# Turning the normed rows of two tiles in place, and a lower rate for the finish: a decoder layer on one core

## The chip, the cores and the metric

The kernel runs on one core of one Trainium2 chip. The core has TensorE (matrix products and transposes), VectorE, ScalarE and GpSimd, an on-chip memory of 128 partitions, and PSUM, where TensorE leaves its results in banks of 128 x 512 numbers. Transfers between the on-chip memory and DRAM run on 16 DMA engines; this kernel issues them from SyncE's queue (SP) and from ScalarE's. The metric is the device time of one execution in microseconds (us); lower is better.

## The reference

The kernel computes one decoder layer on 2048 rows of 1024 numbers, in float32. Cut to what matters:

```python
hn = rms_norm(h, mix_pre_g)
proj = hn @ w_in                                  # q, k, v and the input of a convolution group
attn_out = sliding_window_attention(q, k, v, attn_sinks, rel_bias)
conv_out = conformer_conv(u, ...)                 # GLU, 31 causal taps, LayerNorm, swish, pointwise
mixed = concatenate([attn_out, conv_out]) @ w_out
h = h + rms_norm(mixed, mix_post_g)
hn = rms_norm(h, ffn_pre_g)                       # the "normed rows" of this change
ff = (silu(hn @ w_gate) * (hn @ w_up)) @ w_down
h = h + rms_norm(ff, ffn_post_g)
```

with `rms_norm(x, g) = x * rsqrt(mean(x*x) + eps) * g`.

## The kernel before

**Tiles and stages.** The 2048 rows go in four tiles of 512 (tile 0 to 3), each of four blocks of 128 rows. A name carries its stage: `hl@G` is a buffer of the pool `hl` written in stage G. The stages are

- A: input projections of a tile; B: its attention; C: its convolution. The 31 taps of C run on VectorE over a long time, `stage_tail` does the rest.
- U: the pointwise weights are folded into the output projection, once.
- W (`stage_w`, lines 693 to 745): output projection of a tile in two groups of four 128-column blocks of the mixed rows. `norm_w` (747 to 784) follows: it scales the result, adds x, stores h to `h_scr`, takes the second mean square and writes the normed rows into `xs`, four buffers of the pool `chl`. Each block of normed rows then goes to DRAM (`hn_scr`, line 783) on ScalarE's queue.
- H (`stage_h_plain`, 824 to 835, and `stage_h_sums`, 837 to 867): the normed rows have to stand with their columns on the partitions. `turned` (806 to 811) loads a column block of a tile from `hn_scr` (`load_cols`, line 788: 128 partitions x 4 pieces of 128 numbers) and turns it on TensorE in four transposes into one PSUM bank. `stage_h_plain` does this for the first tile of a pair (0 or 2): copy with the gain into a buffer of `gb`, store that to `hT` (line 831), then split into a high part (ScalarE, line 833) and a low part (VectorE, `lo`). It makes the operands B11 (column blocks 0 to 3) and B21 (4 to 7). `stage_h_sums` reads `hT` of the first tile back, turns the second tile of the pair (1 or 3) and makes the other operands.
- F (`stage_pre`, `stage_p1`): gate and up projections of a pair of tiles by a seven-product scheme of Strassen's kind; `stage_pre` does the products that need only B11 and B21. G (`stage_p2`): the down projection of the pair, in seven types of product, each over eleven steps; the splits of its operands are `hl@G` (line 792). When a type is complete, results for a pair of blocks go to `finish` (1088 to 1108): squares (ScalarE, L1094), products with the gain (GpSimd), a load of h from `h_scr` (L1102) into `chl` (first pair), the sum and the stores to `out`.

All products are in three parts (high x high, high x low, low x high).

**Order.** The program is written as generators that yield a pace in us. One main line (A0 to A3, W1, F, G, F, G) drives clocks, and beside it run lanes: `lw` (W0, and during the first pair's G: C2, W2, C3, W3, B11.2, then N3, the norm of tile 3), `lh` (H of the pairs), `lf` (finishes), `lc` (taps), and others. Each lane has a rate, which may depend on the name of the item at its head (`rates`): an item that yields 2.0 at a rate of 1.25 takes 1.6 us of the main line. `until` runs a lane's items to the end of the named one at once. This fixes the order in which instructions are emitted; a planner then orders each engine's queue by emission priority and by its own estimate of when data and buffers are there, so an instruction may run well ahead of its place in the program. On the chip each engine, and each of the queues, works in order: a DMA issue that waits holds back what is behind it on its engine.

**Buffers that the change touches.** `chl` has five buffers: in `norm_w` one holds the gain and four hold `xs`; W's second group, `finish` and `stage_h_sums` use the same pool. `gb` has two (the turned row on its way to `hT`), `ct` is one PSUM bank (turned blocks of C and of H's first tiles), `fa` four, `fc` three, `at` two.

**Where W0 and W2 lie.** W0 with its norm ends with A3, right ahead of W1, which is the main line's next item; W1's second group waits until eight products of F have run (`Q0 = 8`, line 735 to 740). W2 runs in lane `lw` beside the first pair's G.

Of the kernel before, what the change touches and what calls it, by code (L numbers as in the profile page):

```python
# [12 lines left out]
F32 = mybir.dt.float32  # L13
# [4 lines left out]
AF = mybir.ActivationFunctionType  # L18
# [7 lines left out]
P = 128  # L26
T = 512
NT = S // T
KC = D // P
# [8 lines left out]
def layer_kernel(ctx, tc, x, xT, cols, rows, sinks, relb, onehot, w_in, w_pw, w_out, w_gate, w_up, w_down, out):  # L38
    nc = tc.nc
# [4 lines left out]
    dr = ctx.enter_context(tc.tile_pool(name="dr", bufs=1, space=DRAM))  # L44

    uid = [0]
    lab = ["X0"]
# [7 lines left out]
    def t_(tag, shape, dt=F32):  # L55
        return sb.tile(list(shape), dt, tag=tag, name=nm(tag), bufs=BUFS[tag])

    def f4(tag, shape=(P, D)):
        return t_(tag, shape)

    def f2(tag, shape=(P, T)):
        return t_(tag, shape)

    def hl(tag):
        return t_(tag, (P, 2, T), F32R)

    def sm(n, dt=F32):
        kind = "A" if lab[0][0] == "G" else lab[0][0]
        return sb.tile([P, 8], dt, tag="sm" + kind, name=nm("sm"), bufs=16)[:, 0:n]

    def bank(tag, bufs):
        return ps.tile([P, T], F32, tag=tag, name=nm(tag), bufs=bufs)
# [3 lines left out]
    ct = lambda: bank("ct", 1)  # L76


    act = nc.scalar.activation
# [54 lines left out]
    def weight(src, low, made, raw=None, on_pool=True):  # L134
        if raw is None:
            raw = t_("raw", (P, 2, T))
            nc.sync.dma_start(raw, src)
        return [split_w(raw[:, n], "w", low[n], made, on_pool) for n in range(2)]
# [55 lines left out]
    ident = cst.tile([P, P], F32, name="ident")  # L194
# [16 lines left out]
    g_ffn = colt[:, 8:16]  # L211
# [29 lines left out]
    glu_scr = dr.tile([4, P, S], F32, name="glu_scr")  # L241
    hn_scr = dr.tile([S, D], F32, name="hn_scr")
    y_scr = dr.tile([4, P, S], F32, name="y_scr")
    qs = {}
    started = set()

# [433 lines left out]
    def block_half(acc, units, n, first, L, bank_of, s0=0):  # L680
        cs = slice(n * T, (n + 1) * T)
        for i in range(len(acc)):
            s = i + s0
            lab[0] = L
            o = bank_of()
            three(o, [((a[s // 4][:, 0, ss(s)], a[s // 4][:, 1, ss(s)]), (w[:, 0], w[:, 1])) for a, w in units])
            if first:
                act(acc[i][:, cs], o, AF.Copy)
            else:
                vtt(acc[i][:, cs], acc[i][:, cs], o, ALU.add)  # L690
            yield 0.65 * len(units)

    def stage_w(w, atag, htags, rtags, bank_of, norm=None, ready=None):
        G = KC // len(htags)
        L = f"W{w}"
        lab[0] = L
        acc = [f4(atag) for _ in range(4)]

        def acts(gi):
            aa = []  # L700
            lab[0] = L
            n = 4 if rtags[gi] == "yt" else 2
            for c in range(G * gi, G * gi + G, n):
                ms = t_(rtags[gi], (P, n, T))
                nc.sync.dma_start(ms, mixT[c : c + n, :, w * T : (w + 1) * T].rearrange("c p t -> p c t"))
                for j in range(n):
                    a = hl(htags[gi])
                    act(a[:, 0], ms[:, j], AF.Copy)
                    vtt(a[:, 1], ms[:, j], a[:, 0].bitcast(F32), ALU.subtract)
                    aa.append([a])  # L710
            return aa

        def weights(gi, n):
            ws = []
            for c in range(G * gi, G * gi + G, 2):
                if c < 4:
                    ws += weight(w_out[c : c + 2, :, n * T : (n + 1) * T].rearrange("c p t -> p c t"), lo_out[n, c : c + 2], w > 0, on_pool=False)
                else:
                    for j in range(2):
                        ws.append(hl("w"))  # L720
                        nc.sync.dma_start(ws[-1].bitcast(F32), fold[n, c - 4 + j])
            return ws

        nxt = acts(0)
        yield W_LEAD
        for gi in range(KC // G):
            aa = nxt
            for n in range(2):
                lab[0] = L
                if n == 1 and gi + 1 < KC // G and not (ready and G * gi + G == 4):  # L730
                    nxt = acts(gi + 1)
                ws = weights(gi, n)
                yield from block_half(acc, list(zip(aa, ws)), n, gi == 0, L, bank_of)
            if ready and G * gi + G == 4:
                for i, c in enumerate(ready()):
                    if i == Q0 // 2:
                        ld.until("C1")
                        lab[0] = L
                        nxt = acts(gi + 1)
                    yield c  # L740
        tail = norm_w(w, acc)
        if norm:
            norm(tail)
        else:
            yield from tail

    def norm_w(w, acc):
        L = f"W{w}"
        lab[0] = L

        def whole(src):
            t = f4("chl")
            nc.sync.dma_start(t, src)
            return t

        gb = whole(rows[0].partition_broadcast(P))
        ssq = sm(4)
        for s in range(4):
            act(junk, acc[s], AF.Square, accum_out=ssq[:, s : s + 1])
            yield 0.75  # L760
            lab[0] = L
        r = rsqrt(ssq, 4, D, w < 3)
        xs = [whole(x[w * T + s * P : w * T + (s + 1) * P]) for s in range(4)]
        ssq2 = sm(4)
        yield 3
        for s in range(4):
            lab[0] = L
            stt(acc[s], acc[s], r[:, s : s + 1], gb, ALU.mult, ALU.mult)
            yield 1.25
            lab[0] = L  # L770
            vtt(acc[s], xs[s], acc[s], ALU.add)
            r0 = w * T + s * P
            nc.sync.dma_start(h_scr[r0 : r0 + P], acc[s])
            act(junk, acc[s], AF.Square, accum_out=ssq2[:, s : s + 1])
            yield 1.25
        lab[0] = L
        r2 = rsqrt(ssq2, 4, D, w < 3)
        yield 3
        for s in range(4):
            lab[0] = L  # L780
            act(xs[s], acc[s], AF.Copy, scale=r2[:, s : s + 1])
            r0 = w * T + s * P
            nc.scalar.dma_start(hn_scr[r0 : r0 + P], xs[s])
            yield 1.25

    def load_cols(w, k, tag):
        t = f2(tag, (P, 4, P))
        nc.sync.dma_start(t, hn_scr[w * T : (w + 1) * T, k * P : (k + 1) * P].rearrange("(s p) c -> p s c", p=P))
        return t
# [5 lines left out]
    def lo(x, w, on_pool):  # L795
        (ptt if on_pool else vtt)(w[:, 1], x, w[:, 0].bitcast(F32), ALU.subtract)
# [7 lines left out]
    COLTAG = {0: ["fc", "at", "fc", "at"], 2: ["fc", "at", "fc", "at"]}  # L804

    def turned(w, k, bank_of, tag):
        c = load_cols(w, k, tag)
        b = bank_of()
        for s in range(4):
            nc.tensor.transpose(b[:, s * P : (s + 1) * P], c[:, s], ident)  # L810
        return b

    def op_tile(ws, ops, n, k, spare):
        tag = OPTAG[ws[0]][n][k]
        if tag == "yt":
            if "yt" not in spare:
                spare["yt"] = t_("yt", (P, 2, 2, T), F32R)
            w = spare["yt"][:, k]
        else:
            w = hl(tag)  # L820
        ops.setdefault(n, []).append(w)
        return w

    def stage_h_plain(ws, ops, n, off):
        L = f"H{ws[0]}"
        for k in range(4):
            lab[0] = L
            b = turned(ws[0], k + off, ct, COLTAG[ws[0]][k] if ws[0] else "fa")
            u = f2("gb")
            act(u, b, AF.Copy, scale=g_ffn[:, k + off : k + off + 1])  # L830
            nc.scalar.dma_start(hT[ws[0] // 2][k + off], u)
            o = op_tile(ws, ops, n, k, {})
            act(o[:, 0], u, AF.Copy)
            lo(u, o, False)
            yield 2.0
# [499 lines left out]
    lf = Lane(1.2, 0)  # L1335
    lh = Lane(1.2, 0)
# [2 lines left out]
    ld = Lane(2.0, 0)  # L1339
    lanes = [lb, lc, lu, lw, ld, lf, lh, lt]  # L1340
    lh.rates = {"N1": 1.2, "S0": 0.9, "H0": 1.2}
    lc.rates = {"T0": RC0, "T1": RC1, "T2": RC2, "T3": RP}
    lw.rates = {"W0": RW0, "C2": RW, "W2": RW, "C3": RW, "W3": RW}

# [57 lines left out]
            hn_a[t + 1] += split_x(t + 1, xa[t + 1][0], xa[t + 1][2], range(4, KC))  # L1402
    lw.until("W0")
    mids = [dr.tile([7, NF // 2, P, T], F32, name=f"mids{i}") for i in range(2)]
    hT = [dr.tile([KC, P, T], F32, name=f"hT{i}") for i in range(2)]
    td = dr.tile([4, NF // 2, P, T], F32, name="td")
    keeps = [dr.tile([PRES[2 * i], P, T], F32, name=f"keeps{i}") for i in range(2)]
    ws, ops = (0, 1), {}
# [12 lines left out]
    ws, ops = (2, 3), {}  # L1421
# [76 lines left out]
```

## Time and profile before

| | |
|---|---|
| time, median of 3 runs | 1985.41 us (1983.29, 1985.41, 1989.40) |
| profiled execution | 1988.67 us; its span in the trace 1986.6 us |
| mean granted clock of TensorE in it | 0.992 |
| busiest engines, share of the span | TensorE 97%, VectorE 73%, ScalarE 48%, GpSimd 17% |
| moved by DMA | 454.56 MB, mean 229 GB/s |
| DMA packets | 229403, of them under 512 B 22632, under 2 KB 48400 |
| stores to hn_scr | 16 of 512 KB, from 476.8 to 1297.7 us |
| loads from hn_scr for tile 0 | 8 of 256 KB into `fa`, from 489.1 to 518.2 us |

How to read it: times are from the start of the span. In a row of a timeline stand start, length, engine, line, operation, `out<-in`, shape and count; a bracket gives the idle time ahead of it and what ended that. SPq and ACTq are the queues' DMA issues, which are not counted as busy. In the waits, a row is the waiting instruction, what it waited for, total us, number of times and the longest. In the DMA issues, the last number is the median time from issue to landing.

### The profile page before, as it was taken

The numbers are of one execution on the slowest core, as the hardware profiler recorded it, in microseconds if no ns is written. First come the engines' busy times: TensorE is split into PE (matmuls) and PEld (weight loads), VectorE is DVE, ScalarE is ACT, GpSimd is POOL, SyncE is SP. The second block draws the span as 40 slices with busy tenths as digits, with TensorE's granted clock in tenths as the row PEclk, the third lists the DMA queues.
The fourth block names the chain that finished last, engine by engine and source line by source line (L and its number), as shares of the span: only waits on it lengthen the run. The fifth ranks groups of instructions, "written<-read, shape, count | busy, mean of one in ns | idle before, by whom it ended". The sixth has DMA issues, their size and how long they took to land.

```text
span 1986.6 us, 26669 instructions
## 1 busy us (share of the span) xinstructions
PE 1930.2 (97%) x8730; PEld 1542.3 (78%) x8730; DVE 1460.2 (73%) x2578; ACT 955.2 (48%) x1878; POOL 336.4 (17%) x415
## 2 busy tenths in 40 slices
PE   8999999998999999899999999989999999999997
PEld 6777767776777778778888778768888888888886
DVE  5999969986875898888658975766666665455557
ACT  5455454436737633334355466556634433345443
POOL 4011111003121200000000110144423332311003
PEclk9999999999999999999999999989999999999999
DMA  8797757669659867885477788797844542466664
GB/s 312 253 316 234 228 176 242 213 198 306 203 191 353 290 216 237 285 267 181 154 236 251 266 302 282 270 315 244 289 149 165 170 164 81 143 232 194 210 196 144
DMA packets 229403, 454.56 MB, mean 229 GB/s; under 512 B 22632, under 2 KB 48400, under 8 KB 229264
## 3 DMA queue, kind: packets, MB, share of 16 engines
q1 hardware_dynamic: 211024, 426.64, 64.5%
q10 hardware_dynamic: 18240, 26.22, 3.6%
q8 instruction: 69, 1.13, 0.2%
q14 instruction: 70, 0.57, 0.1%
HBM read 331.65 MB, written 121.12 MB: 228 GB/s over the span
## 4 chain that ended last, share of the span: by engine, by line
PE 43%; DMA 10%; DVE 9%; issue 3%; POOL 2%; ACT 2%; SPq 1%; DVEq 0%; ACTq 0%; POOLq 0%
PE mm@F L85 29%; PE mm@G L85 12%; DVE fc@C L94 2%; PE tr@W L85 2%; DMA gb@F<-keeps 1%; DVE hl@G L94 1%; DMA mids<-fa@F 1%; DMA fa@G<-mids 1%; DMA td<-fc@G 1%; DVE w@F L94 1%; DMA fc@G<-w_down 1%; DMA wx@G<-w_down 1%; DVE fa@F L94 1%; DVE chl@F L94 1%; DMA mixT<-fc@C 1%
## 5 line engine op out<-in xcount | busy, mean ns | idle before, releaser
L94 DVE SCALAR_TENSOR_TENSOR fc@C<-glu@C,colt,fc@C 128x512 f32<-128x512 f32 x480 | 356.5, 760 | 2.9
L85 PE MATMUL mm@F<-hl@H,w@F 128*128 128x512 f32 x1056 | 253.0, 390 | 3.3 <-ACT mm@F L919 2.0
L85 PE MATMUL mm@G<-hl@G,hl@G 128*128 128x512 f32 x924 | 232.6, 397 | 11.2 <-ACT hl@G L792 7.7
L85 PEld LDWEIGHTS mm@F<-hl@H,w@F 128*128 128x128 f32 x1056 | 197.5, 188 | 46.3 <-ACT mm@F L919 3.7
L85 PEld LDWEIGHTS mm@G<-hl@G,hl@G 128*128 128x128 f32 x924 | 173.0, 190 | 51.7 <-ACT hl@G L792 9.0
L85 PE MATMUL mm@A<-hl@A,w@A 128*128 128x512 f32 x840 | 206.5, 395 | 4.2 <-ACT w@A L127 1.9
L792 ACT ACTIVATE w@F<-chl@F 128x512 fp32r<-128x512 f32 x220 | 135.4, 625 | 142.1 <-PE mm@F L85 131.5
L85 PE MATMUL mm@G<-w@G,hl@G 128*128 128x512 f32 x876 | 199.4, 389 | 0.0
L85 PEld LDWEIGHTS mm@G<-w@G,hl@G 128*128 128x128 f32 x876 | 164.4, 188 | 34.1
L85 PEld LDWEIGHTS mm@A<-hl@A,w@A 128*128 128x128 f32 x840 | 155.4, 188 | 42.2 <-ACT w@A L127 2.6
L94 DVE TENSOR_TENSOR w@F<-chl@F,w@F 128x512 fp32r<-128x512 f32 x198 | 144.8, 735 | 35.9 <-ACT w@F L792 35.3
L85 PE MATMUL mm@F<-ql@H,w@F 128*128 128x512 f32 x528 | 128.4, 391 | 9.2 <-ACT mm@F L1026 5.0
L85 PE MATMUL mm@F<-mid@H,w@F 128*128 128x512 f32 x528 | 131.7, 396 | 0.0
L85 PE MATMUL mm@F<-p@H,w@F 128*128 128x512 f32 x528 | 129.4, 390 | 0.0
L85 PE MATMUL mm@F<-x@H,w@F 128*128 128x512 f32 x528 | 125.7, 391 | 0.0
L85 PEld LDWEIGHTS mm@F<-ql@H,w@F 128*128 128x128 f32 x528 | 98.8, 188 | 31.6 <-ACT mm@F L1026 6.4
L494 POOL TENSOR_SCALAR_AFFINE_SELECT p@B<-p@B 128x512 f32<-128x512 f32 x62 | 57.6, 938 | 374.0 <-ACT p@B L492 372.7
L85 PEld LDWEIGHTS mm@F<-mid@H,w@F 128*128 128x128 f32 x528 | 100.0, 190 | 21.9 <-ACT fa@F L1047 0.5
L85 PEld LDWEIGHTS mm@F<-p@H,w@F 128*128 128x128 f32 x528 | 99.5, 188 | 21.0 <-ACT at@F L1040 0.2
L85 PEld LDWEIGHTS mm@F<-x@H,w@F 128*128 128x128 f32 x528 | 98.6, 188 | 21.5 <-issue 0.8
L127 ACT ACTIVATE w@A<-raw@A 128x512 fp32r<-128x512 f32 x110 | 67.4, 625 | 93.5 <-PE mm@A L85 54.8
L94 DVE TENSOR_TENSOR w@G<-raw@G,w@G 128x512 fp32r<-128x512 f32 x73 | 51.5, 705 | 68.1 <-ACT w@G L792 66.8
(302 smaller groups left out, 3300.6 us busy)
## 6 DMA issues: line engine op xcount, KB each, us to landing
mids<-fa@F SPq DMA_DIRECT2D x154, 256.0 KB, 2.8
raw@A<-w_in SPq DMA_DIRECT2D x55, 512.0 KB, 4.7
w@A<-lo_in SPq DMA_DIRECT2D x84, 256.0 KB, 3.6
fc@G<-mids SPq DMA_DIRECT2D x77, 256.0 KB, 3.5
fa@G<-mids SPq DMA_DIRECT2D x75, 256.0 KB, 4.6
gb@F<-keeps SPq DMA_DIRECT2D x72, 256.0 KB, 3.9
w@W<-fold SPq DMA_DIRECT2D x32, 512.0 KB, 5.1
chl@F<-w_gate SPq DMA_DIRECT2D x22, 512.0 KB, 4.1
```

The source lines that it names most:

```text
L85: r = nc.tensor.matmul(*args, **kw)
L94: r = op(*args, **kw)
L127: act(w[:, 0], raw, AF.Copy)
L494: nc.gpsimd.affine_select(out=pg[:, kb].rearrange("p (i q) -> p i q", q=P), in_=pg[:, 1].rearrange("p (i q) -> p i q", q=P), compare_op=AL ...
L792: act(w[:, 0], x, AF.Copy)
```

## The change

Three things change.

1. Tile 0: `norm_w` no longer stores the normed rows to `hn_scr` (only odd tiles do). The four `chl` buffers are kept in `normed`, and `stage_h_plain` turns each column block straight from them (`turn_row`): four transposes into `ct`, one copy with the gain into `gb`, one store to `hT`, as before, but without the load. In `stage_w` of tile 1, B21.0 is run to its end ahead of the second group's splits, which want `chl`.
2. Tile 2: its eight column blocks are turned at the end of `norm_w(2)` in lane `lw`, 2.0 of pace each, and go to `hT` only. `stage_h_plain` of the second pair then loads each block from `hT` in place of turning it; the split stays.
3. Lane `lf`: the finishes of the first pair (O0.1, O0.3, E0.1, E0.3) run at a rate of 0.5 in place of 1.2; 1.2 is set again for the others.

Tiles 1 and 3 keep their way through `hn_scr`. `hT` is allocated earlier, without effect of its own.

```diff
+    hT = [dr.tile([KC, P, T], F32, name=f"hT{i}") for i in range(2)]
...
                     if i == Q0 // 2:
                         ld.until("C1")
+                        lh.until("B21.0")
                         lab[0] = L
                         nxt = acts(gi + 1)
...
             act(xs[s], acc[s], AF.Copy, scale=r2[:, s : s + 1])
-            r0 = w * T + s * P
-            nc.scalar.dma_start(hn_scr[r0 : r0 + P], xs[s])
+            if w % 2:
+                r0 = w * T + s * P
+                nc.scalar.dma_start(hn_scr[r0 : r0 + P], xs[s])
             yield 1.25
+        if w == 0:
+            normed.extend(xs)
+        if w == 2:
+            for k in range(KC):
+                turn_row(w, xs, k)
+                yield 2.0
+
+    normed = []
+
+    def turn_row(w, xs, k):
+        lab[0] = f"H{w}"
+        b = ct()
+        for s in range(4):
+            nc.tensor.transpose(b[:, s * P : (s + 1) * P], xs[s][:, k * P : (k + 1) * P], ident)
+        u = f2("gb")
+        act(u, b, AF.Copy, scale=g_ffn[:, k : k + 1])
+        nc.scalar.dma_start(hT[w // 2][k], u)
+        return u
...
         for k in range(4):
             lab[0] = L
-            b = turned(ws[0], k + off, ct, COLTAG[ws[0]][k] if ws[0] else "fa")
-            u = f2("gb")
-            act(u, b, AF.Copy, scale=g_ffn[:, k + off : k + off + 1])
-            nc.scalar.dma_start(hT[ws[0] // 2][k + off], u)
+            if ws[0]:
+                u = f2(COLTAG[ws[0]][k])
+                nc.sync.dma_start(u, hT[ws[0] // 2][k + off])
+            else:
+                u = turn_row(0, normed, k + off)
+                lab[0] = L
             o = op_tile(ws, ops, n, k, {})
             act(o[:, 0], u, AF.Copy)
             lo(u, o, False)
...
+    lf.rates = {n: 0.5 for n in ("O0.1", "O0.3", "E0.1", "E0.3")} | {n: 1.2 for n in ("Y0", "Y1", "O2.1", "O2.3")}
...
-    hT = [dr.tile([KC, P, T], F32, name=f"hT{i}") for i in range(2)]
```

## The prediction

> **What bounds the kernel now.** I read the page first, then the timeline of TensorE over the whole span for its idle stretches, then the same stretches on the other engines, in the stretch table and in the waits.
>
> ```profile
> PE 1930.2 (97%) x8730; PEld 1542.3 (78%) x8730; DVE 1460.2 (73%) x2578; ACT 955.2 (48%) x1878; POOL 336.4 (17%) x415
> ```
>
> TensorE is busy for 1930.2 of 1986.6 us, so all its idle time is 56 us, and the change takes no product away. It can gain only where TensorE stands still. Two long holes, the longest after the start, lie where the change works (timeline of TensorE: start, length, line, operation, count, and in brackets the idle time before):
>
> ```profile
> 491.45 1.65 PE L85 MATMUL tr@B<-kz,ql@A 64*128 64x256 f32 x12 [5.59 <-DVE sm@B L454]
> 493.03 7.45 PE L85 MATMUL mm@W<-w@W,hl@W 128*128 128x512 f32 x28
> 502.91 4.86 PE L85 MATMUL mm@W<-w@W,hl@W 128*128 128x512 f32 x20
> 510.22 0.97 PE L85 MATMUL tr@B<-kz,ql@A 64*128 64x256 f32 x11
> ...
> 1318.33 8.49 PE L85 MATMUL mm@G<-hl@G,hl@G 128*128 128x512 f32 x24 [6.50 <-ACT hl@G L792]
> 1328.90 5.74 PE L85 MATMUL mm@G<-hl@G,hl@G 128*128 128x512 f32 x24
> 1335.52 7.55 PE L85 MATMUL mm@G<-hl@G,hl@G 128*128 128x512 f32 x32 [0.88 <-DVE hl@G L94]
> ```
>
> After each hole the products run slowly for a while; the stretch table shows why. Its columns: stretch, length, busy time of TensorE, weight load, VectorE, ScalarE and GpSimd, then the granted clock, the DMA share and GB/s.
>
> ```profile
> 484.00:488.00 4.00, 1.87 (x17) 1.26 (x15) 3.93 (x7) 1.12 (x2) 0.00 (x0) 0.99 1.03 395
> 488.00:492.00 4.00, 0.55 (x4) 0.58 (x6) 4.00 (x15) 1.31 (x3) 0.00 (x0) 0.50 1.04 382
> 492.00:496.00 4.00, 4.00 (x21) 3.23 (x18) 3.96 (x8) 0.88 (x2) 0.00 (x0) 0.66 1.13 332
> ...
> 1312.00:1316.00 4.00, 0.00 (x0) 0.00 (x0) 0.00 (x0) 0.62 (x2) 0.00 (x0) 0.74 1.08 365
> 1316.00:1320.00 4.00, 1.67 (x4) 1.40 (x5) 3.34 (x3) 4.00 (x12) 3.82 (x4) 0.50 1.09 355
> 1320.00:1324.00 4.00, 4.00 (x10) 3.12 (x10) 3.90 (x7) 3.36 (x9) 3.83 (x6) 0.50 0.77 213
> ```
>
> The clock falls to 0.50. The 28 products at 493.03 take 7.45 us; at the later 4.86 / 20 = 0.243 us each they would take 6.80, and 12 of tr@B at 0.97 / 11 each 1.06 instead of 1.65: 1.24 us lost. The 24 products at 1318.33 lose 8.49 - 5.74 = 2.75. So the first hole is worth 5.59 + 1.24 = 6.83 us, the second 6.50 + 2.75 = 9.25, and the small one at 1335.52 another 0.88: 16.96 us for everything in reach. In both holes the DMA share is above 1.00: the transfers are the queue.
>
> **The first hole, tile 0.** What goes here: four stores to hn_scr on ScalarE's queue and eight loads from it on SP's. The 32 transposes, eight copies and eight hT stores stay.
>
> ```profile
> 476.84 0.34 ACTq L783 DMA_DIRECT2D hn_scr<-chl@W  x1
> 480.59 0.67 ACTq L783 DMA_DIRECT2D hn_scr<-chl@W  x1
> ...
> 476.66 0.38 SPq L607 DMA_DIRECT2D mixT<-fc@C  x1
> 480.55 0.37 SPq L705 DMA_DIRECT2D yt@W<-mixT  x1
> ...
> 483.66 0.55 DVE L94 TENSOR_SCALAR fc@C<-glu@C,colt 128x512 f32<-128x512 f32 x1 [7.43 <-DMA mixT<-fc@C]
> 490.69 2.19 ACT L708 ACTIVATE hl@W<-yt@W 128x512 fp32r<-128x512 f32 x4 [4.69 <-DMA yt@W<-mixT]
> ...
> hn_scr<-chl@W ACTq DMA_DIRECT2D x16, 512.0 KB, 6.7
> mixT<-fc@C SPq DMA_DIRECT2D x16, 256.0 KB, 5.2
> yt@W<-mixT SPq DMA_DIRECT2D x4, 1024.0 KB, 5.8
> hT<-gb@H ACTq DMA_DIRECT2D x16, 256.0 KB, 4.4
> ```
>
> The four stores are 2.1 MB, at 390 GB/s 5.4 us of all DMA engines, between 476.8 and 480.6. In the same time the store that VectorE waits for (its fc buffer) takes 483.66 - 476.66 = 7.0 us, 1.8 over its median, and the load that W1's products wait for takes 490.69 - 480.55 = 10.1 us, 4.3 over its median. Without the stores I set both at their medians: VectorE goes on 1.8 us sooner and gives TensorE its tr bank 1.8 us sooner.
>
> The rows are ready by 480, so the transposes may go into the hole instead of into the crowded time from 500 on (the first two rows below, of TensorE and of the stretch table, are a short hole from elsewhere):
>
> ```profile
> 803.93 1.66 PE L85 MATMUL mm@F<-yt@H,w@F 128*128 128x512 f32 x6 [1.65 <-DVE gb@F L94]
> ...
> 806.00:810.00 4.00, 4.00 (x20) 3.27 (x18) 4.00 (x7) 0.00 (x0) 0.00 (x0) 1.00 0.70 196
> ...
> 507.60 0.60 PE L810 MATMUL ct@H<-ident,fa@H 128*128 128x128 f32 x4
> 509.55 0.69 ACT L830 ACTIVATE gb@H<-ct@H,colt 128x512 f32<-128x512 f32 x1
> ```
>
> One turned row costs 0.60 us on TensorE, 4.8 us in all. There is one ct bank and there are two gb buffers, each held until its hT store has landed (4.4 us), so I let three rows into the hole: 1.8 us. The hole shrinks to 5.59 - 1.8 - 1.8 = 2.0 us. A hole of 1.65 us, the nearest, is followed by a clock of 1.00, so I charge none: -3.6 - 1.24 = **-4.8 us**. Bounds: 0 if the earlier hT stores fill the gap that the hn_scr stores leave, -6.83 if the hole closes; a loss only by the third rival. ScalarE saves four issues. The four chl buffers stay taken until the eighth row is turned; behind them waits only W1's second split, whose products come after eight products of the next stage (8 x 2.76 us in the code's own pace). The forced end of B21.0 ahead of that split finds it done: 16 units at rate 1.2 are 13.3 us, against 4 + 20.8 us of pace before that point. Both cost nothing; without that cover the price is a row's whole turn, 0.60 + 0.69 + 4.4 = 5.7 us.
>
> In the Trainium skill (TensorE: Matmul & The Clock Gate, section "What's actually happening") an idle window of about 3.4 us halves the array's clock, and a busy one restores it. The trace agrees: 5.59 and 6.50 us of idling end at 0.50. By that rule a rest of 2.0 us keeps the clock; were both rests just over the window, the 1.24 + 2.75 us would stay and the sum below would be -5.8.
>
> **The second hole, the end of the first pair's down projection.** What moves here: the H2 rows B11 and B21 lose their transposes, copies and hT stores; each becomes one load, one copy and one subtraction. And the finish of the first pair is emitted at 0.5 in place of 1.2.
>
> ```profile
> 1302.88 0.62 ACT L792 ACTIVATE hl@G<-fa@G 128x512 fp32r<-128x512 f32 x1
> 1308.79 0.67 ACT L830 ACTIVATE gb@H<-ct@H,colt 128x512 f32<-128x512 f32 x1
> 1315.01 0.33 ACTq L831 DMA_DIRECT2D hT<-gb@H  x1
> 1315.38 0.63 ACT L1094 ACTIVATE junk<-p@G 128x512 bf16<-128x512 f32 x1 [5.92 <-DMA chl@G<-h_scr]
> 1317.14 0.61 ACT L792 ACTIVATE hl@G<-mb@G 128x512 fp32r<-128x512 f32 x1
> ...
> 1304.05 1.44 SPq L1133 DMA_DIRECT2D mb@G<-w_down  x2
> 1306.06 0.45 SPq L1102 DMA_DIRECT2D chl@G<-h_scr  x1
> 1311.90 1.25 SPq L1133 DMA_DIRECT2D mb@G<-w_down  x2
> ...
> SPq L1102 <- DMA hn_scr<-chl@W: 7.7, 3, 6.6
> ```
>
> ScalarE finished the copy of an H2 row at 1309.46 and could not issue its hT store until 1315.01, when the finish's load of h (issued at 1306.06) had landed. Behind that issue stood the splits hl@G that TensorE wanted; none ran from 1303.5 to 1317.14. With the store gone ScalarE is there 5.55 us sooner, the hole falls to 0.95 us and the 2.75 us of slow clock go: -8.3. What is late next is the data: SP stood 6.6 us with a finish load at its head, waiting for a chl buffer of tile 3's hn_scr store, which the change keeps, and the weights issued at 1311.90 come late whatever ScalarE does. I give 2.3 us back for that: **-6 us**. Bounds: 0 if another wait stands in the same place, -10.13 if both holes here close. The lower rate puts these finish loads behind more weight loads in the order, which is on the gaining side. It hides nothing late: a finish is 8 units, 16 us at 0.5; the two that start with the last products end 32 us later, while the sums that want their x and p buffers are emitted 16 x 2.76 = 44 us into the next stage. Without that cover they would take the cover of the remaining 16 products, another 44 us.
>
> **The added place, tile 2's rows.** Eight rows now follow the norm of tile 2: 32 transposes (only moved), eight copies of 0.69 us and eight hT stores on ScalarE, in the middle of the down projection, while four hn_scr stores go. Behind them in that lane stand C3 and W3, whose results have until the end of the stage.
>
> ```profile
> 1170.41 2.19 ACT L781 ACTIVATE chl@W<-mid@W,sm@W 128x1024 f32<-128x1024 f32 x2 [6.36 <-POOL sm@W L156]
> 1175.16 0.63 ACT L792 ACTIVATE hl@G<-mb@G 128x512 fp32r<-128x512 f32 x1 [0.48 <-ACT chl@W L781]
> 1176.37 1.53 PE L85 MATMUL mm@G<-hl@G,hl@G 128*128 128x512 f32 x4 [0.60 <-ACT hl@G L792]
> ```
>
> Here ScalarE made no hl@G for 6.36 + 4.75 = 11.1 us and TensorE lost 0.60. So a held store costs little: I take **+1 us**. Bounds: 0, and +7.8 from the third rival. At this place 2.1 MB of hT stores stand for 2.1 MB of hn_scr stores; later the loads are as large as before and 2.1 MB of stores are gone.
>
> The Trainium skill (DMA: Bandwidth & Descriptors, "Anatomy of one DMA") says that a transfer's wait is served on the sequencer that issues it. That speaks against the change: the 5.55 us hold only moves with the stores to 1175. By the row above a hold of that length there costs at most 0.60, so the sum by the rule is 0.4 us lower.
>
> **Sum.** -4.8 - 6 + 1 = -9.8 us. The profiled execution took 1988.67 us (its span of 1986.6 and 2.1 around it), which gives 1978.9; it lies 3.3 above the median of 1985.41, against which the forecast is 1975.6, put down as 1976.
>
> **The rivals.**
>
> *The change does not reach the second hole.* The finish's pieces run when their data is there, whatever their rate: the planner may put the same loads at SP's head and ScalarE waits for something else, a load of hT for instance. For it: the row that waits 6.6 us for tile 3's store, which stays. Against it: the 5.55 us are those of a store that goes. Then -4.8 + 1: 1981.6.
>
> *Both holes close, and the three rows in the first are five or more.* For it: the DMA share over 1.00 in both, with 2.1 MB taken from the first. Against: hT stores move into the first. Then -17 + 1: 1969.4.
>
> *Rows outrun their buffers (the slower one).* The code paces a row at 2.0 / 1.25 = 1.6 us (tile 2) or 2.0 / 1.2 = 1.7 (tile 0); on the chip a row's turn of 5.7 us in two gb buffers gives one row per 2.9. Once rows are no longer thinned by loads from DRAM, ScalarE stops at the third copy, TensorE stops at the next transpose, which stands at the head of its queue and waits for the one ct bank, and the products behind it wait too. Price: 6 rows x 1.3 = 7.8 us for tile 2 and 6 x 1.2 = 7.2 for tile 0, whose gain goes; with -6 at the end: +9, 1994.4. It decides from a landing time of about 2.5 us (2 x 1.6 - 0.69), and 4.4 is beyond that. Against it: the planner counts these stores too, and where rows now follow each other within 3.5 us TensorE does not wait.
>
> **How the numbers follow.** The forecast 0.45 (its own range 1971 to 1982), not reaching the second hole 0.22, both closed 0.15, slower 0.18. What a measurement of this kernel tells from no change is about 0.3%, 6 us: 1979.5 to 1991.4. Faster: 0.8 of 0.45, all of 0.15, 0.2 of 0.22: 0.55. Slower: 0.18 and 0.01 of the forecast: 0.19. The rest, 0.26, is within. The range goes from 1966, somewhat below the second rival, to 1995, just past the third.
>
> **What would show it.** No idle stretch above 3 us on TensorE near 486 and near 1312, and no stretch of clock 0.50 behind them; VectorE's wait for mixT<-fc@C near 476 about 5 us; 6.3 MB less moved by DMA (4.2 less for each tile, 2.1 more for tile 2's loads); rows of tile 0 turned from 481 on. Wrong would be: TensorE waiting for ScalarE's copy at a transpose of a row (third rival), or the same 6 us hole at the end of the down projection (first).

## The result, and the profile after

| | before | after |
|---|---|---|
| time, median | 1986.33 us (1983.29 to 1989.40, 4 runs) | 2015.78 us (2013.50 to 2017.90, 4 runs) |
| profiled execution, span | 1986.6 us | 2011.8 us |
| mean granted clock of TensorE | 0.992 | 0.987 |
| moved by DMA | 454.56 MB | 448.25 MB |

The ratio is 1.0152, 95% interval 1.0135 to 1.0169: the change costs about 30 us. The forecast was 1976 us, the range 1966 to 1995.

Line numbers after the change are about 20 higher from line 800 on: the split hl@G and w@F is now L813, the seed copy mm@F L942, the copy fa@F L964 and its store to `keeps` L965, the finish's squares L1117 and its load of h L1125; L801 to L804 are the new `turn_row`.

Both holes are gone, and the time is lost elsewhere. To see where, I cut the span at three places that are easy to find in TensorE's timeline: the first product of the first pair's gate and up projections ("F0"), the first of its down projection ("G0") and of the second pair's gate and up projections ("F2").

| us | F0 starts | F0 lasts | G0 lasts | F2 lasts | N3's normed rows start |
|---|---|---|---|---|---|
| before | 521.88 | 491.07 | 330.23 | 418.71 | 1293.40 |
| after | 512.09 | 505.67 | 316.18 | 453.05 | 1349.99 |
| difference | -9.79 | +14.60 | -14.05 | +34.34 | +56.59 |

(N3 is the norm of tile 3. A stage ends where the next begins.) The sum of the four differences is +25.1 of the 25.2 us by which the spans differ. Each of the two gains is there, and each is given back, and more, in the stage behind it.

The single numbers are larger than what was won and lost, because products also move from one side of a stage's mark to the other. F0 holds 2106 matmuls after and 2090 before, and twelve transposes of tile 3 that lay in G0 lie in F2 after. The sums of two neighbours are safer: the change reaches G0 4.8 us later (1017.76 against 1012.95), and G0 and F2 together take 20.3 us longer.

The stretch table of after at the two old holes, and in the stage that lost most (columns as in the prediction: stretch, length, busy time of TensorE, weight load, VectorE, ScalarE, GpSimd, granted clock, DMA share, GB/s):

```profile
476.00:500.00 24.00, 23.85 (x127) 19.06 (x126) 16.94 (x35) 15.53 (x26) 0.00 (x0) 1.00 0.84 289
...
1290.00:1340.00 50.00, 50.00 (x222) 41.42 (x221) 31.69 (x52) 23.04 (x42) 4.86 (x3) 1.00 0.60 217
1340.00:1400.00 60.00, 47.49 (x202) 37.44 (x201) 41.75 (x74) 33.58 (x72) 32.67 (x42) 0.97 0.97 331
1400.00:1450.00 50.00, 39.84 (x156) 31.48 (x157) 39.49 (x43) 29.77 (x57) 27.91 (x19) 0.86 0.79 268
```

and the same stretches of before:

```profile
476.00:500.00 24.00, 18.41 (x93) 14.99 (x93) 16.46 (x44) 11.53 (x21) 0.00 (x0) 0.86 0.95 331
...
1290.00:1340.00 50.00, 42.55 (x179) 33.46 (x178) 35.23 (x62) 26.31 (x51) 20.64 (x31) 0.90 0.93 314
1340.00:1400.00 60.00, 59.90 (x266) 49.20 (x265) 34.29 (x59) 35.28 (x70) 24.08 (x18) 1.00 0.76 256
1400.00:1450.00 50.00, 50.00 (x230) 41.23 (x229) 38.06 (x51) 31.06 (x57) 19.76 (x14) 1.00 0.75 252
```

Look at GpSimd and at the DMA share. Between 1290 and 1340 GpSimd fell from 20.64 to 4.86 us and the DMA share from 0.93 to 0.60; between 1340 and 1400 GpSimd rose from 24.08 to 32.67 and the DMA share from 0.76 to 0.97. Of GpSimd's 37.5 us between 1290 and 1400 after, 17.4 are the finish's products with the gain. So the work that crowded the end of G0 was not removed, it moved into the start of F2, and TensorE's idle time moved with it: 12.51 us idle before 1400 and 10.16 after it, where before there was 0.10.

TensorE's timeline in that stage shows no single big hole but seven of 2.4 to 3.4 us between 1370 and 1426, most of them ahead of a product of 12 or 24 matmuls. Six of them:

```profile
1373.54 3.04 PE L85 MATMUL mm@F<-ql@H,w@F 128*128 128x512 f32 x12 [2.79 <-ACT fa@F L964]
...
1390.49 2.56 PE L85 MATMUL mm@F<-mid@H,w@F 128*128 128x512 f32 x10 [3.35 <-DVE w@F L94]
1396.80 3.06 PE L85 MATMUL mm@F<-mid@H,w@F 128*128 128x512 f32 x12 [2.87 <-ACT mm@F L942]
1402.61 1.21 PE L85 MATMUL mm@F<-mid@H,w@F 128*128 128x512 f32 x2 [2.76 <-ACT mm@F L942]
...
1413.13 7.22 PE L85 MATMUL mm@F<-mid@H,w@F 128*128 128x512 f32 x24 [2.76 <-ACT mm@F L942]
...
1425.27 7.39 PE L85 MATMUL mm@F<-mid@H,w@F 128*128 128x512 f32 x24 [2.77 <-ACT mm@F L942]
```

They wait for ScalarE in three ways: for a copy that empties a bank (fa@F, L964), for a seed of a bank (L942), and for a split of weights, whose low part VectorE makes from ScalarE's high part (w@F). ScalarE's own timeline says why it is late:

```profile
1370.40 0.33 ACTq L965 DMA_DIRECT2D keeps<-fa@F  x1
1370.77 0.63 ACT L1117 ACTIVATE junk<-x@G 128x512 bf16<-128x512 f32 x1 [4.56 <-DMA chl@G<-h_scr]
...
1388.40 0.59 ACT L964 ACTIVATE fa@F<-mm@F 128x512 f32<-128x512 f32 x1
1395.77 0.33 ACTq L965 DMA_DIRECT2D keeps<-fa@F  x1
1396.14 0.60 ACT L942 ACTIVATE mm@F<-gb@F 128x512 f32<-128x512 f32 x1 [7.15 <-DMA raw@F<-w_up]
```

The squares of the finish (L1117) stand between the copies of F2, and twice ScalarE stands still for long before it issues a store to `keeps`, 4.56 and 7.15 us, while the DMA engines are full (a share of 1.04 from 1366 to 1371 and 1.00 from 1388.5 to 1396). It is the picture that the prediction read at 1315 in the kernel before, 55 and 80 us later.

What is late is the whole second half of the lane that makes tile 3. The one bank `ct` shows where it begins. TensorE's turns after:

```profile
1184.13 0.60 PE L801 MATMUL ct@H<-ident,chl@W 128*128 128x128 f32 x4
1184.48 5.49 PE L85 MATMUL mm@G<-hl@G,hl@G 128*128 128x512 f32 x23
1189.82 0.60 PE L801 MATMUL ct@H<-ident,chl@W 128*128 128x128 f32 x4
...
1218.31 0.60 PE L801 MATMUL ct@H<-ident,chl@W 128*128 128x128 f32 x4
1223.99 0.60 PE L550 MATMUL ct@C<-ident,fc@C 128*128 128x128 f32 x4
```

and before:

```profile
1125.38 0.60 PE L549 MATMUL ct@C<-ident,fc@C 128*128 128x128 f32 x4
1134.69 0.60 PE L549 MATMUL ct@C<-ident,fc@C 128*128 128x128 f32 x4
1139.72 0.60 PE L549 MATMUL ct@C<-ident,fc@C 128*128 128x128 f32 x4
```

The first of tile 2's eight rows comes at 1175.9, and from the second, at 1184.13, one comes every 5.7 us. The first turn of C3, the convolution of tile 3, comes behind the last of them, at 1223.99; before, it came at 1125.38, and three turns of C3 stood ahead of tile 2's norm.

The 5.7 us are not a wait on the chip. ScalarE's copy of the second row was

```profile
1184.77 0.69 ACT L803 ACTIVATE gb@H<-ct@H,colt 128x512 f32<-128x512 f32 x1 [1.56 <-PE ct@H L801]
```

so the bank was empty again at 1185.46, 4.4 us ahead of the third row's transposes, and TensorE ran products without a hole in that time. The rows stand that far apart in TensorE's queue, in the order that the planner wrote. How it comes to 5.7 us the runs don't show, only that the number of banks matters to it (e5, e12).

C3 feeds W3, W3 feeds N3, and N3's rows go to DRAM 57 us later.

### The profile page after: what moved, and what is told of

Read it like the earlier page. It is cut to its first block, busy times and chain, and to the rows that moved or that the text cites. A ratio compares the mean times of both kernels' runs of the same rounds, so it can differ in the third digit from the quotient of the medians.

```text
span 2011.8 us, 26656 instructions
## 1 busy us (share of the span) xinstructions
PE 1939.4 (96%) x8730; PEld 1550.8 (77%) x8730; DVE 1463.8 (73%) x2578; ACT 953.9 (47%) x1878; POOL 335.4 (17%) x415
## 2 busy tenths in 40 slices
DMA packets 220954, 448.25 MB, mean 223 GB/s; under 512 B 22376, under 2 KB 39952, under 8 KB 220816
## 4 chain that ended last, share of the span: by engine, by line
PE 47%; DMA 9%; DVE 5%; issue 2%; ACT 2%; POOL 1%; SPq 1%; ACTq 0%; DVEq 0%; POOLq 0%
PE mm@F L85 24%; PE mm@G L85 19%; PE tr@W L85 4%; DMA gb@F<-keeps 2%; DMA td<-fc@G 1%; DMA chl@F<-w_gate 1%; DVE fa@F L94 1%; DMA fc@G<-w_down 1%; DVE w@F L94 1%; DVE chl@F L94 1%; DVE fc@C L94 1%; DMA mids<-fa@F 1%; DMA wx@G<-w_down 1%; DMA chl@G<-h_scr 0%; DMA raw@F<-w_up 0%
## 5 line engine op out<-in xcount | busy, mean ns | idle before, releaser
L813 ACT ACTIVATE w@F<-chl@F 128x512 fp32r<-128x512 f32 x220 | 135.0, 625 | 116.6 <-PE mm@F L85 109.6
L85 PE MATMUL mm@F<-mid@H,w@F 128*128 128x512 f32 x528 | 137.6, 407 | 17.6 <-ACT mm@F L942 11.2
```

The costliest lines, as they stand in the source:

```text
L85: r = nc.tensor.matmul(*args, **kw)
L813: act(w[:, 0], x, AF.Copy)
```

## The experiments

Theory A: tile 2's rows hold `ct` ahead of C3; C3, W3 and N3 come late, and with the finishes that wait for them in the queues they fall on the first products of F2. Theory B: the finish at 0.5 puts its work into F2. Theory C: any change of the emission order costs some 25 us, wherever it is. "Before" in each is the kernel before, on the same chip.

**Each part alone.**

e1_tile0: the kernel after, with tile 2 back on its old way and the old rate.

```diff
-            if w % 2:
+            if w:
...
-        if w == 2:
-            for k in range(KC):
-                turn_row(w, xs, k)
-                yield 2.0
```

> Part 1 alone: tile 0 turned in place, tile 2 through DRAM as before, finish rate 1.2. Theory A (the loss comes from tile 2's rows, which hold the one ct bank ahead of C3, so that the norm of tile 3 comes 57 us later, into the second pair's F): the first hole closes as in the changed kernel (F starts near 512 instead of 522), part of it is lost again in F, no hole after 1340: 1975 to 1990 us, N3's rows near 1290. Theory B (the finish at 0.5 is the loss): the same here. Theory C (any change of the order costs some 25 us somewhere in F): 2000 or more.

Measured: 1992.85 us, ratio 1.0029 (1.0019 to 1.0040). F0 started at 512.36, F0 lasted 505.28, F2 418.78, N3's rows started at 1297.48. The time is just above the 1975 to 1990 of theory A. So tile 0's part costs 5 to 6 us by itself: the first hole closes and F0 takes it back. One trace of each kernel shows this stage only roughly: of six kernels with tile 0's part as in the change, five reach G0 between 1017.3 and 1022.5 us and e5 at 1011.94; of six with tile 0's old way and no other edit to it, five between 1011.4 and 1013.0 and e2 at 1017.15.

e2_tile2: tile 2's part alone.

```diff
-            if w % 2:
+            if w != 2:
...
-                u = turn_row(0, normed, k + off)
-                lab[0] = L
+                b = turned(0, k + off, ct, "fa")
```

> Part 2 alone: tile 2 turned at the end of its norm, tile 0 through DRAM as before, finish rate 1.2. Theory A: rows one per 5.7 us, C3's turns only after the eighth, N3's rows near 1355, the hole at the end of the first G closed, 20 to 35 us lost in the second pair's F: 2000 to 2015 us. Theory B: no loss in F without the lower rate: 1975 to 1985.

Measured: 2011.22 us, ratio 1.0111 (1.0088 to 1.0135); N3's rows at 1348.43, F2 452.84. The row of its stretch table has the loss of after:

```profile
1340.00:1400.00 60.00, 47.72 (x196) 37.18 (x194) 42.88 (x75) 33.86 (x74) 32.22 (x43) 0.94 0.96 335
```

e3_rate: the rate 0.5 alone, added to the kernel before (the added line of the change).

> Part 3 alone: the kernel before with the first pair's finish at 0.5. Theory A: the finish has time when N3 is early: 1978 to 1990 us. Theory B: the h loads and squares of the finish move into F and hold SP and ScalarE there: 2005 to 2020.

Measured: 1988.37 us, ratio 0.9998 (0.9987 to 1.0010). The second hole is still there, 6.15 us ahead of 1317.80.

e4_no_rate: the change without the line of rates.

> The changed kernel with the finish's rate back at 1.2 (parts 1 and 2). Theory A: still 2005 to 2020 us, since N3 stays late. Theory B: back to 1975 to 1990 us.

Measured: 2012.82 us, ratio 1.0125 (1.0108 to 1.0142); N3's rows at 1351.03, F2 454.12. By these four, B falls (the rate does nothing alone, and without it e4 still lies 25 us over its before, where the change lies 29 over its own), C falls (tile 0's part also changes the order and costs 5 to 6 us), and most of the loss sits in tile 2's part. By the medians the three parts alone cost 5.2, 23.6 and 0.8 us; their sum, 29.6, is about the 29.5 of the change.

**Is it the bank, the rows, or the lateness?**

e5_tr: one edit to the kernel after.

```diff
-        b = ct()
+        b = tr() if w else ct()
```

> The kernel after the change, with one edit: tile 2's eight rows are turned on the rotating banks tr in place of the one bank ct, so C3's turns need not stand behind them. Theory A (the rows hold the one ct bank ahead of C3, so C3, W3 and N3 come 57 us late and fall with the finishes into the second pair's first products): N3's normed-row copies start by 1305 (1293.4 before, 1350.0 after), no string of idles of 2 to 3.4 us on TensorE between 1368 and 1425, the second pair's stage from 1334 on takes about what it took before (453 us instead of 487), time 1982 to 1995. Rival D (the rows' own copies and hT stores on ScalarE, or loads of hT in place of transposes in the second pair, cost the time wherever C3 stands): 2008 to 2018, the string of idles stays.

Measured: 1998.83 us, ratio 1.0063 (1.0040 to 1.0086). N3's rows started at 1298.37 and F2 lasted 418.75 us: the string of holes is gone, as A expects, and about half of the loss with it: 13.9 us over its before remain of 29.5. (The lengths in the expectation, 453 and 487, do not fit the table: this stage took 418.71 us before and 453.05 after.) The time is above the expected 1982 to 1995. In the trace G0 lasted 335.35 us, longer than the 330.23 of before. But the profiled execution took 1992.7 us, the shortest of its five, so the trace doesn't show where the other 6 us up to the median lie.

e6_t2_tr: tile 2's part with the same edit, the rest as before.

> Tile 2's part alone with the rows on the banks tr; tile 0 and the finish's rate as before. Theory A: the hole at the end of the first pair's down projection is gone (second pair starts at about 1333 against 1343) and nothing is given back: 1975 to 1985, faster than before by 2 to 10 us. Rival D: as e2_tile2, 2006 to 2014.

Measured: 1993.98 us, ratio 1.0045 (1.0032 to 1.0058). F2 lasted 418.76, as A expects; F0 491.39, as before. But the gain that I expected at the end of G0 did not come: G0 lasted 335.70, and the time, 9 us over before, lies in neither range. So tile 2's rows cost something of their own without any lateness of N3, some 5 us of G0. This is the run that says most of the second hole, so here are its rows. ScalarE's timeline, then TensorE's:

```profile
1316.32 0.63 ACT L810 ACTIVATE hl@G<-mb@G 128x512 fp32r<-128x512 f32 x1 [4.08 <-DMA mb@G<-w_down]
...
1324.90 0.63 ACT L810 ACTIVATE hl@G<-mb@G 128x512 fp32r<-128x512 f32 x1 [3.65 <-DMA mb@G<-w_down]
```

```profile
1160.25 10.08 PE L85 MATMUL mm@G<-hl@G,hl@G 128*128 128x512 f32 x36 [3.07 <-ACT p@G L1182]
1186.43 0.66 PE L798 MATMUL tr@H<-ident,chl@W 128*128 128x128 f32 x4 [2.00 <-ACT gb@H L800]
...
1314.41 10.94 PE L85 MATMUL mm@G<-hl@G,hl@G 128*128 128x512 f32 x40 [2.01 <-DVE hl@G L94]
1330.87 4.60 PE L85 MATMUL mm@G<-hl@G,hl@G 128*128 128x512 f32 x12 [2.34 <-DVE hl@G L94]
```

ScalarE is no longer held by an hT store, and now waits 4.08 and 3.65 us for weights: the transfers were the queue, as the prediction read from the DMA share, and are it still (a share of 1.01 from 1310 to 1318 and 1.07 from 1318 to 1331). The hole of 6.50 is now two of 2.01 and 2.34, and holes of 3.07 and 2.00 us have come at 1160 and 1186. The one of 3.07 lies ahead of tile 2's rows, and what brought it is not shown. The one of 2.00 is a row's transpose that waits for ScalarE's copy of an earlier row, and these copies wait for an hT store to free a `gb` buffer:

```profile
1193.60 0.69 ACT L800 ACTIVATE gb@H<-tr@H,colt 128x512 f32<-128x512 f32 x1 [2.50 <-DMA hT<-gb@H]
```

e7_delay: the kernel before, with nothing moved and a pause in the lane.

```diff
             nc.scalar.dma_start(hn_scr[r0 : r0 + P], xs[s])
             yield 1.25
+        if w == 2:
+            for k in range(36):
+                yield 2.0
```

> The kernel before with nothing moved: after the norm of tile 2 its lane only takes a pause of 36 x 2.0 units, which issues no instruction, so that C3, W3 and N3 come some 50 to 60 us later; the rows go by hn_scr as before and nothing of tile 2 touches ct early. Theory A (the lateness of N3 alone is the cost): the same string of idles in the second pair's first products, 2005 to 2022. Rival D (the rows' instructions are the cost): 1982 to 1993.

Measured: 2002.68 us, ratio 1.0074 (1.0050 to 1.0098). No instruction differs from the kernel before in kind or number, only when tile 3 is made: N3's rows at 1344.23, F2 437.81. The median lies just under the range I gave, far from the rival's. TensorE's timeline has the same string, less dense:

```profile
1373.65 8.41 PE L85 MATMUL mm@F<-ql@H,w@F 128*128 128x512 f32 x24 [3.27 <-ACT fa@F L944]
1389.50 0.76 PE L85 MATMUL mm@F<-ql@H,w@F 128*128 128x512 f32 x1 [2.52 <-ACT w@F L795]
```

So a late lane costs 19 us of F2 with no added instruction. But the pause does not delay N3 alone. Tile 2's rows on their old way come late with it: six are copied between 1302.84 and 1340.82, and the last two fall well into F2, where ScalarE issues their stores some 5 us after the copies:

```profile
1362.16 0.33 ACTq L834 DMA_DIRECT2D hT<-gb@H  x1
...
1371.47 0.44 ACTq L834 DMA_DIRECT2D hT<-gb@H  x1
```

The hole of 3.27 stands right behind the second of these. So this run by itself doesn't separate N3 from the rows. The others do: after the change the last of the rows' stores was issued at 1219.67 and the string came (N3 at 1349.99), and in e5 the same rows, with N3 at 1298.37, brought none. Rival D falls as the cause of the string; the rows' own 5 us in G0 (e6) stay. In e7 the finishes did not move either (GpSimd worked 138.18 us in F2, 137.47 before, 158.50 after), so theory A's finishes are not needed for a string of holes.

e11_delay_short: the same with 20 in place of 36.

> As e7_delay with a pause of 20 x 2.0 units in place of 36 x 2.0: a second point for theory A. If the lateness of N3 costs by degrees: N3's copies start between 1305 and 1335, the second pair's stage (418.7 us when N3 starts before 1300, 437.8 in e7 at 1344) takes 420 to 434, time 1986 to 2000. If any lateness breaks the order: as e7, 1997 to 2008.

Measured: 1988.70 us, ratio 1.0015 (1.0001 to 1.0030); N3's rows at 1310.87, F2 422.06. The numbers lie in the ranges for a cost by degrees, but the trace says otherwise. In F2 TensorE stood still for 0.07 of the 422.06 us, at a clock of 1.00; the 3.35 us more are busy time, with the twelve transposes that lay in G0 before. G0 and F2 together took 1.9 us longer, against 15.1 in e7. So N3 can come 17 us late without one hole in F2, and at 45 us late or more (e8, e7, e2) the string is there. Where between the two it begins no run shows.

e8_rows_behind_C3: the change with tile 2's rows as an item of the lane behind C3.

```diff
-            for k in range(KC):
-                turn_row(w, xs, k)
-                yield 2.0
+            normed[:] = xs
...
+    lw.add("R2", rows_2())
     lw.add("W3", stage_w(3, "mid", ["ql", "chl"], ["chl", "yt"], tr, norm=lambda g: lw.add("N3", g)))
```

> The kernel after the change, with tile 2's rows on ct as there, but as an item of the lane behind C3 and ahead of W3: C3's turns come as early as before, W3 and N3 still stand behind the rows. Theory A with N3 as the thing that is late: N3's copies start between 1305 and 1345 and the time is in between, 1992 to 2010. Theory A with C3's own output as the thing that is late: 1982 to 1992. Rival D: 2008 to 2018.

Measured: 2006.85 us, ratio 1.0094 (1.0068 to 1.0120). C3's first turn came at 1130.93, nearly as early as before, tile 2's last hT store at 1274.48, and N3's rows still only at 1338.51; F2 lasted 443.22. So C3 need not be late for the loss, and the rows cost nearly as much behind it as ahead of it (22 us over before against 29). What is late in all these runs is what stands behind the rows, W3 and N3; the two are not separated.

e12_pace: the change with the rows' own pace at a quarter.

```diff
                 turn_row(w, xs, k)
-                yield 2.0
+                yield 0.5
```

> The kernel after the change with the pace of tile 2's rows at 0.5 in place of 2.0 units a row. If the one ct bank sets their distance, the rows' transposes stay 5.7 us apart, N3's copies start at 1347 to 1353 and the time is that of the change, 2009 to 2020. If the written pace sets it (8 rows x 1.5 / 1.25 = 9.6 us), the rows come closer together, N3 starts by about 1340 and the time falls to 1998 to 2008.

Measured: 2010.62 us, ratio 1.0107 (1.0068 to 1.0146). TensorE's turns stay as far apart as they were:

```profile
1201.24 0.60 PE L801 MATMUL ct@H<-ident,chl@W 128*128 128x128 f32 x4
1207.19 0.60 PE L801 MATMUL ct@H<-ident,chl@W 128*128 128x128 f32 x4
1212.90 0.60 PE L801 MATMUL ct@H<-ident,chl@W 128*128 128x128 f32 x4
```

From the second row on they are 5.3 to 6.0 us apart. N3's rows started at 1355.90, later than the 1347 to 1353 expected (the norm of tile 2 was 7 us later too), and F2 lasted 448.78. On the banks `tr` (e5) the eight rows' transposes lay between 1170 and 1192. So the distance goes with the number of banks, through the planner's order, and not with the written pace.

**Why F0 gives the first hole back.** In e1 a load stood at the head of SP's queue for 8.3 us, the first read of hT in `stage_h_sums`, which wants a `chl` buffer; before, it was 4.5 us:

```profile
SPq L866 <- DVE mid@W L94: 8.3, 1, 8.3
```

e9_t0_own: e1 with this load in a buffer that is idle then.

```diff
-            own = t_("chl", (P, 2, T))
+            own = t_("wx" if k == 0 and ws[0] == 0 else "chl", (P, 2, T))
```

> Tile 0's part alone (e1_tile0), with one edit: the first load of hT in the first pair's stage takes the idle wx buffer in place of a chl buffer, so it need not wait for VectorE's sum mid@W. In e1 this load stood at the head of SP's queue for 8.3 us (590 to 598) with the weights of the first pair behind it, while DMA stood still from 593 to 596. Theory F (this hold gives back the first hole's gain): SP's wait there below 1 us, the 5 us hole at 619 below 2 us, the first pair's stage from its first product to the down projection's first (505.3 us in e1, 491.1 before) at most 499, time 1976 to 1987. Rival G (the volume of transfers between 600 and 660, at a DMA share of 1.0, is the limit, in whatever order): the stage stays at 502 to 508, time 1988 to 1996.

Measured: 1989.12 us, ratio 1.0018 (1.0004 to 1.0032). The hold did not go, it passed to the next instruction on SP:

```profile
SPq L775 <- DVE mid@W L94: 10.3, 3, 8.2
```

F0 lasted 494.32, but it also started 7 us later than in e1, at 519.48: 23 matmuls fewer lie in it (2082 against 2105), and a row of tile 0 now waits 1.75 us ahead of 486.69 for the norm's copy. G0 was reached at 1013.80, 3.8 us sooner than in e1. The hole of e1 at 624.17, 4.55 us, is now 1.34 ahead of 623.19, with another of 1.70 ahead of 630.61. By F0's length theory F is right, by the time rival G.

e10_before_own: the same edit alone, on the kernel before.

> The kernel before with the same edit alone (the first hT load into wx). There the load held SP for 4.5 us. Theory F: 1 to 5 us faster than before, 1980 to 1986. Rival G: no difference, 1985 to 1990.

Measured: 1990.80 us, ratio 1.0024 (1.0011 to 1.0038): slower, which neither theory had. F0 lasted 498.15. So this edit tells nothing between F and G; the buffer of one load moves the time by 5 us, and why e1's F0 gives back its gain is not settled by it. None of the kernels is faster than the one before; e3, the rate alone, equals it.

## Why the prediction was wrong, point by point

**Tile 2's rows: the step that failed.** The prediction set +1 us, with bounds 0 and +7.8, and said of C3 and W3 behind them in the lane that their "results have until the end of the stage". They have some slack, at least the 17 us of e11, but not the 57 that they came late. In the kernel before, N3's rows start 25 us ahead of the end of the second hole (1293.40 against 1318.33), and behind N3 come B21.2 and S2; the finishes' loads stand on SP among them. All that stands in ScalarE's and SP's queues, which F2 wants for itself. The price was 34.34 us in F2, 20.3 when the shorter G0 is set against it. It is shown by e2 (19.1 in G0 and F2 with tile 2's part alone) and by e5 (the same rows without the lateness: F2 back at 418.75, and 5.2 left in G0 and F2); e7 agrees (15.1 for a late lane without a row added). I costed the rows by what ScalarE and TensorE do for them and took the lane behind them to have slack, without reading when its last item ends.

The prediction worked out 5.7 us for a row's turn and used it for buffers; eight of them are 46 us, and N3 came 56.6 us later. That would have been near by luck: its 5.7 us are 0.60 + 0.69 us and the 4.4 until an hT store lands, while the bank was free again 4.4 us ahead of the next row, and the 5.7 us of the trace are the planner's order.

**The second hole: not gained.** The prediction set -6, for an hT store that no longer holds ScalarE. After, G0 is 14.05 us shorter, which looks like a confirmation with a bonus. It isn't: with N3 at its old time (e5, e6) G0 lasts 335.4 and 335.7 us against 330.2, and in e6 the weights are late by 4.08 and 3.65 us. The 14 us came with N3's stores and the finishes leaving the stretch. N3's leaving is not enough: in e7 it leaves too, the finishes and tile 2's old rows stay, and a hole of 7.64 us stands ahead of 1333.19. "What is late next is the data" was the right sentence, with 2.3 us as its price. In e6 the waits at the end of G0 (2.01, 2.34 and 1.44 us) and the new holes at 1160 and 1186 took more than the gain. The rival that the change does not reach the second hole came nearest to e5 and e6, though it had no loss.

All the signs that the prediction named came true, to within a few us: no hole near 486 or 1312, a wait of 5.28 us for fc, 6.3 MB less. They test whether the holes close, and none of them looks at the stages behind.

**The first hole: right, and of no use.** VectorE's wait for its fc buffer fell from 7.43 us to

```profile
480.73 0.55 DVE L94 TENSOR_SCALAR fc@C<-glu@C,colt 128x512 f32<-128x512 f32 x1 [5.28 <-DMA mixT<-fc@C]
```

(5.6 by the prediction), the first row turned at 484.89 (481), 0.15 us of idle is left between 476 and 500, and the clock stays at 1.00. F0 started 9.79 us sooner against 4.8 forecast, in part because sixteen matmuls more now lie behind its first product. Then F0 lasted 14.60 us longer: TensorE was busy 7.6 us longer in it, with those matmuls and at a lower clock, and stood still 7.0 us longer. The prediction had no term for that: it carried a gain ahead of F0 straight to the end. TensorE's rows by stretch, before and after:

```profile
600.00:660.00 60.00, 56.66 (x260) 45.62 (x259) 39.32 (x54) 44.58 (x76) 12.77 (x20) 1.00 0.97 334
...
750.00:850.00 100.00, 94.29 (x405) 76.51 (x405) 85.52 (x139) 34.92 (x62) 0.00 (x0) 0.98 0.80 265
```

```profile
600.00:660.00 60.00, 50.47 (x214) 40.84 (x213) 34.73 (x52) 41.09 (x71) 14.96 (x20) 0.91 0.93 324
...
750.00:850.00 100.00, 91.53 (x383) 74.24 (x382) 81.40 (x132) 33.15 (x60) 0.00 (x0) 0.95 0.77 255
```

Idle time grew by 6.2 and 2.8 us in these two stretches, and the clock fell. In 600 to 660 tile 1's norm, its stores and its turning come with F0's weights. In e1 that norm's stores started at 616.34, against 617.41 before: F0 came 9.5 us sooner, tile 1 only 1. That the transfers there (a DMA share of 0.93 to 0.97) set the pace is an argument, not shown; e9 and e10 left it open.

**The rate: right that it costs nothing.** Alone, 0.5 hides nothing late and brings nothing (e3: 0.9998); with the other parts no difference is clear (e4's interval, 1.0108 to 1.0142, and the change's, 1.0135 to 1.0169, overlap).

**The slower rival** had the right sign and the wrong mechanism. It expected rows 1.6 us apart, running into two gb buffers, with TensorE stopped at a row's transpose. With the one bank the planner spread the rows to 5.7 us, so TensorE was not stopped there at all; what stood behind the rows was late instead. Its bound of 1994.4 set the upper end of the range, 20 us short. On the banks `tr`, where rows do come close together, its mechanism is seen: ScalarE's copies wait for hT stores, and TensorE stops once at a row's transpose, 1.01 us in e5 and 2.00 in e6.

**Volume: right.** 454.56 - 448.25 = 6.3 MB less moved, and it bought nothing: the DMA share was 0.93 between 1290 and 1340 before, and 0.97 between 1340 and 1400 after.

## What to carry to other kernels

Where a change adds work to a lane that runs in order, ask of the last item behind it, not of the next one: when does it end now, what starts after it, and how much is left between. A resource with one copy (here one PSUM bank) is used in the order of the program, so added uses stand ahead of all later ones: here eight turns, each of which held the bank for 1.3 us, stood 5.7 us apart in the planned order, and the lane behind them came 45 to 63 us late, though TensorE never stood waiting for the bank. And when a hole closes, check that the work around it was removed rather than moved: compare the busy time of the other engines and the DMA share in the same stretch.

## What the runs showed of the hardware

In F2 after the change the granted clock fell behind idles below 3 us. After idles of 2.79 us (ahead of 1373.54) and 2.38 us (ahead of 1378.95), with 3 us of products between them, the stretch table of after has:

```profile
1374.00:1378.00 4.00, 2.58 (x12) 1.76 (x10) 3.72 (x12) 2.26 (x8) 3.52 (x9) 1.00 0.93 293
1378.00:1382.00 4.00, 3.05 (x7) 2.47 (x8) 3.65 (x8) 3.60 (x9) 3.75 (x7) 0.60 1.13 339
```

The Trainium skill (TensorE: Matmul & The Clock Gate, "What's actually happening") names an idle window of about 3.4 us. The trace agrees only in part: 2.38 to 2.79 us, close together, were enough here, while after a single idle of 3.35 us (ahead of 1390.49) the clock stayed at 1.00 until 1400. A string of small holes so costs more than its idle time: from 1400 to 1450 the clock averaged 0.86, against 1.00 before.
